# Sample block choice emitted before the last four projection tiles, key tiles first, and attention buffers placed in the normed input's tiles

## The chip, the cores and the metric

The kernel runs on one NeuronCore of a Trainium2 chip, as one program. Its engines are TensorE (PE: matmuls and transposes, fed by its own queue of weight loads, PEld), VectorE (DVE), ScalarE (ACT), GpSimd (POOL) and SyncE (SP, which here only issues transfers). ACT, SP and POOL each have a queue of DMA issues. The metric is the device time of one execution in microseconds (us); lower is better. The time before is the median of three executions.

## The reference, cut to what matters

One layer of a hybrid decoder is computed for 512 prompt tokens (one fresh sequence) and 8 samples of 4 new tokens each, whose past of 2048 tokens lies in page pools:

```python
x = x + 0.5 * swiglu1(rms_norm(x))             # FFN 1
z = rms_norm(x) @ w_in                         # one projection, columns split among the groups
o_nsa = nsa(z[..., :NSA_COLS])                 # 8 query heads in 2 groups, 2 K/V heads
o_rw  = rwkv7(z[..., NSA_COLS:])
x = x + concat([o_nsa, o_rw]) @ w_out
x = x + 0.5 * swiglu2(rms_norm(x))             # FFN 2
y = rms_norm_final(x)
```

The attention group has three branches, merged by sigmoid gates, each with a relative-position bias. The branch over compressed blocks attends to one K/V row for every 64 tokens, made by a small MLP. Its probabilities, summed over a group's heads, are the *importance* by which 16 blocks of 64 tokens are chosen for the second branch. The third is a window of 512 tokens:

```python
_, idx = lax.top_k(score, min(TOP_K_BLOCKS, n_blocks))   # score: importance; first and newest blocks forced
k_sel = gather_sample_blocks(cache_slc_k, ks, idx, page_table)
o_slc = slc_attend(q, pos, k_sel, v_sel, idx, valid, table)
```

For the prompt there are only 8 blocks, so all are chosen and no choice is computed.

## The kernel before

Numbers are fp32. Large products are made of three products of a high and a low part: `hh*wh + hl*wh + hh*wl` (`dense`, L152 to L155). The weights of a tile come in raw on SP's queue (`wload`, L137: tile `wraw`, three buffers of pool `wp`), ACT casts the high part `wh`, DVE subtracts to get the low part `wl`, three buffers each. The normed input lies in `hh` and `hl` (pool `hp`), 8 blocks of rows each.

The stages follow one another: FFN 1, `mix` (L338: input projection, RWKV group, attention group, output projection), FFN 2. In `mix` the attention group's projection goes tile by tile (`nsa_in`, L411) in the order of `ZORD`: 0 to 3 are queries, 4 and 5 the keys and values to be compressed, 10 the gates, then 6 and 8 the keys (selected branch, window) and 7 and 9 the values. A key tile is split into high and low parts `kk` for prompt scores (ACT L445, DVE L446). A value tile is transposed on PE (L434) into `vr`. Each of the four leaves the samples' 32 columns in `new`, by a copy on POOL (L428).

After tile 10 `prompt_cmp` computes the prompt's compressed branch (`PcmT`, `vcd`), then the last four tiles 7, 9, 6, 8 run. `attention_setup` follows: last product of the compression MLP (`hid`, `kccT`), query matrix `qb`, transposes of `new` into `vn`. `attention` (L947) runs two generators by turns: `sample_attn` (lane p) and `prompt_attn` (lane q), whichever is due by the costs that they yield (`STEP`). Their matmuls and transposes go through `mm` and `tr` (L949, L952), which keep the order in which they are written; where nothing is kept, the framework's scheduler orders each engine.

`sample_attn` first computes the samples' compressed scores and softmax (`Pc`), the importance `imp` (L1042), and its ranks, by four blocks of comparisons of all pairs (`gg`, L1065 to L1070, sums `cnt`), which give the mask `mb`. Then for each half of the samples, `scores(s)` multiplies five pairs of loaded pages with `qb`, DVE adds the mask and finds the minimum (`S`, `mx`, L1116), ACT takes the exponential (L1137), PE transposes (`PT`), and `values` multiplies with the pages. The pages come by `kv_load` (L964): 20 loads of eight 128 x 256 pieces, three as indirect DMAs on POOL (`gather`, L903), five on SP (L997), or as whole rows for the window (L986). `KVS` says into which buffers in turn: two of the attention pool (`kv`), the tiles of `hh` and `hl` once the projection is through, and `ar`.

`prompt_attn` works on 32 units: four blocks of 128 queries (i = 3 to 0), four heads (r) and two branches (b). A unit is scores on PE (`pS`), bias and minimum on DVE (L1350), exponential on ACT, normalising on DVE (L1356), transposes on PE (`pq`, into `PTp` or `PTo`), products with `vr` (`po`). Up to `LAG` = 3 units are scored ahead. The queries `qs` lie in `wl`'s buffers, some scores in `wraw`'s, and some transposed probabilities in `wh`'s. `w_out` splits the mixed rows `on` and `orw`, and runs eight tiles.

Of the kernel before, what the change touches and what calls it, by code (L numbers as in the profile page):

```python
# [17 lines left out]
KT = 8  # L18
# [3 lines left out]
STEP = 3.1  # L22
KVB = 4
ZORD = (0, 1, 2, 3, 4, 5, 10, 7, 9, 6, 8)
KVS = ("kv", "hh", "kv", "hl", "ar")
# [22 lines left out]
class Step:  # L48
# [289 lines left out]
    def mix(self):  # L338
        nc = self.nc
        r = self.norm_end()  # L340
        with ExitStack() as st:
# [533 lines left out]
    def attention_setup(self):  # L875
        nc, I, O = self.nc, self.I, self.O
        c = self.at
        self.on = c.tile([128, 4, 2, HW], F32, name="on")
        hg = self.hid
        nc.scalar.activation(hg, hg, AF.Gelu_apprx_tanh, bias=self.pb)  # L880
        self.kccT = c.tile([128, 8, 32], F32, name="kccT")
        pk = self.ps()
        nc.tensor.matmul(pk, self.w2[0:64], hg[0:64], start=True, stop=True)
        for g in range(2):
            gs = slice(64 * g, 64 * g + 64)
            nc.vector.tensor_copy(self.kccT[gs].rearrange("p n b -> p (n b)"), pk[gs, g:512:2])
        self.qb = c.tile([128, 8, 2, 4, 4], F32, name="qb")
        nc.vector.memset(self.qb, 0.0)
        for g in range(2):
            gs = slice(g * 64, g * 64 + 64)  # L890
            nc.vector.tensor_copy(self.qb[gs, :, g], self.zs[gs].rearrange("p r n t -> p n t r"))
        self.vn = c.tile([32, 2, 128], F32, name="vn")
# [61 lines left out]
    def attention(self, bias, cmp):  # L954
        todo = {"p": self.sample_attn(), "q": self.prompt_attn(self.kk, bias, self.vr, *cmp)}
# [15 lines left out]
    def kv_load(self):  # L971
# [4 lines left out]
        if t == "kv":  # L976
            kv = [self.at.tile([128, 4, 256], F32, name="kv", bufs=KVB) for j in range(2)]
        elif t == "ar":
            kv = [self.un1.tile([128, 4, 256], F32, name="kv", tag="ar%d" % j, bufs=1) for j in range(2)]
        else:  # L980
            x = self.hp.tile([128, 2, 4, 256], F32, name="kv", tag=t)
            kv = [x[:, j] for j in range(2)]
# [16 lines left out]
    def sample_attn(self):  # L999
        nc, I, O = self.nc, self.I, self.O  # L1000
        c, new, vn = self.at, self.new, self.vn
        self.pg = c.tile([1, 80], I32, name="pg")
        nc.sync.dma_start(self.pg, I["pg"])
        self.loaded, self.pairs = 0, []
        for _ in KVS:
            self.kv_load()
# [31 lines left out]
        yield 1  # L1038
        p = self.ps()
        self.mm(p[:, 0:64], gsum, Pf, start=True, stop=True)  # L1040
# [3 lines left out]
        self.tr(p[0:64, 0:128], Pf, self.ident)  # L1044
        PcT = c.tile([64, 128], F32, name="PcT")
        nc.scalar.activation(PcT, p[0:64, 0:128], AF.Copy)
        yield 1
        wb = self.rot.tile([128, 512], F32, name="wb", tag="r", bufs=1)
        nc.gpsimd.tensor_copy(wb[:, 0:384], t31.to_broadcast([128, 384]))
        nc.gpsimd.tensor_copy(wb[:, 384:512], sb[:, 0:128])  # L1050
        nc.gpsimd.tensor_add(wb[:, 0:4], wb[:, 0:4], mwin)
# [24 lines left out]
        yield 1  # L1076
        gr = c.tile([16, 48], F32, name="gr")
        p = self.ps()
        for hf in range(2):
            self.tr(p[0:16, 24 * hf:24 * hf + 24], self.gT[0:24, hf, 0:SW], self.ident[0:24, 0:24])  # L1080
        nc.scalar.activation(gr, p[0:16, 0:48], AF.Copy)
        yield 1
        p = self.ps()
        self.mm(p[:, 0:48], sel, gr, start=True, stop=True)
# [5 lines left out]
        for n in range(8):  # L1090
            for g in range(2):
                self.mm(pv[n // 4 * 32:n // 4 * 32 + 32, n % 4 * 128 + g * 64:n % 4 * 128 + g * 64 + 64],
# [502 lines left out]
```

## Time and profile before

| | |
|---|---|
| time before, median of 3 runs (lowest, highest) | 1404.97 us (1395.78, 1405.24) |
| profiled execution, its own time | 1392.31 us |
| its span in the trace | 1390.5 us |
| PE, DVE, ACT, POOL busy, share of the span | 95%, 51%, 37%, 19% |
| FFN 2, from 932.00 us to the end | 458.50 us |
| last four tiles' end to the first matmul of `w_out` | 783.80 us to 928.05 us |

The span is cut into stretches below. A busy time is the time in which an engine has an instruction running. A wait is idle time of an engine ahead of an instruction, put down to what released it. PEclk is the mean clock that TensorE was granted, as a share of full speed. In a timeline a row is one or several like instructions: start, time from the first's start to the last's end, and in brackets the idle time ahead.

### The profile page before, as it was taken

What the parts mean: (1) busy time and instruction counts of PE and PEld (TensorE: products, weight loads), DVE (VectorE), ACT (ScalarE), POOL (GpSimd) and SP (SyncE); (2) the same over time, 40 slices, a digit from 0 to 9 for tenths busy, and PEclk for the clock granted to TensorE, in tenths of its full rate; (3) what the DMA queues carried; (4) which work ended last, traced back from release to release, by engine and by line L of the source; (5) the groups of instructions that cost most, each with busy time, mean ns of one, the idle gap of its engine ahead of it and who ended that gap; (6) DMA issues with size and microseconds to landing.
All of it is one profiled execution on the core that took longest, in us unless ns stands there. A gap on an engine that the chain in (4) does not pass through costs nothing.

```text
span 1390.5 us, 31672 instructions
## 1 busy us (share of the span) xinstructions
PE 1315.2 (95%) x13313; PEld 1240.6 (89%) x13313; DVE 706.4 (51%) x1357; ACT 512.7 (37%) x925; POOL 258.9 (19%) x317
## 2 busy tenths in 40 slices
PE   6999999999999998998999779989999999999996
PEld 6999999999999977787678667769999999999996
DVE  6443343333333558869685675765544444442224
ACT  5232232233222555451223455754433333332231
POOL 2073567530000111210003214301000000000000
PEclk9999999999999999699999889999999999999998
DMA  4464465544443311112225528625322222233332
GB/s 157 162 197 121 149 201 186 174 132 116 124 118 114 112 54 46 34 41 73 73 78 180 149 72 243 201 79 179 100 92 84 91 86 90 88 100 108 102 105 84
DMA packets 99328, 163.25 MB, mean 117 GB/s; under 512 B 16185, under 2 KB 42881, under 8 KB 98546
## 3 DMA queue, kind: packets, MB, share of 16 engines
q1 hardware_dynamic: 74258, 114.71, 26.8%
q0 software_dynamic: 9040, 25.24, 6.1%
q10 hardware_dynamic: 15888, 21.28, 5.0%
q8 instruction: 105, 1.72, 0.5%
q14 instruction: 37, 0.30, 0.1%
HBM read 150.19 MB, written 16.72 MB: 120 GB/s over the span
## 4 chain that ended last, share of the span: by engine, by line
PE 68%; DVE 6%; ACT 3%; DMA 3%; issue 2%; POOL 0%; SPq 0%; ACTq 0%; DVEq 0%; POOLq 0%
PE acc L155 53%; PE pp L949 1%; PE pq L952 1%; PE po L949 1%; PE pS L949 1%; DMA kv<-in_slc 1%; PE pq L697 1%; PE pp L480 1%; PE pp L581 1%; DMA kv<-in_slc,idx 1%; DVE ivt L636 1%; PE pq L155 1%; PE pq L722 1%; PE pp L859 0%; DMA kv<-in_wkv 0%
## 5 line engine op out<-in xcount | busy, mean ns | idle before, releaser
L155 PE MATMUL acc<-hl,wh 128*128 128x272 f32 x2064 | 427.4, 292 | 3.9 <-ACT wh L146 3.9
L146 ACT ACTIVATE wh<-wraw 128x512 fp32r<-128x512 f32 x338 | 209.7, 621 | 581.9 <-PE acc L155 537.2
L155 PE MATMUL acc<-hh,wh 128*128 128x272 f32 x1808 | 384.1, 293 | 9.1 <-ACT hh L104 9.1
L148 DVE TENSOR_TENSOR wl<-wraw,wh 128x512 fp32r<-128x512 f32 x338 | 232.0, 687 | 306.2 <-ACT wh L146 304.3
L155 PE MATMUL acc<-hh,wl 128*128 128x272 f32 x1808 | 381.3, 292 | 1.6 <-DVE wl L148 1.6
L155 PEld LDWEIGHTS acc<-hl,wh 128*128 128x128 f32 x2064 | 325.3, 191 | 9.4 <-ACT wh L146 4.2
L155 PEld LDWEIGHTS acc<-hh,wh 128*128 128x128 f32 x1808 | 288.1, 190 | 14.5 <-ACT hh L104 9.1
L155 PEld LDWEIGHTS acc<-hh,wl 128*128 128x128 f32 x1808 | 285.5, 190 | 4.4 <-DVE wl L148 1.9
L903 POOL DMA_INDIRECT cp<-in_cmp,idx x128 | 131.1, 1024 | 98.6 <-issue 37.2
L122 POOL TENSOR_TENSOR ss<-ss,sq 128x544 f32<-128x544 f32 x23 | 31.6, 1374 | 612.4 <-ACT sq L118 597.0
L155 PE MATMUL acc<-ah,wh 128*128 128x272 f32 x660 | 136.9, 289 | 0.0
L155 PE MATMUL acc<-al,wh 128*128 128x272 f32 x660 | 136.3, 288 | 0.0
L155 PE MATMUL acc<-ah,wl 128*128 128x272 f32 x660 | 135.6, 286 | 0.0
L155 PEld LDWEIGHTS acc<-al,wh 128*128 128x128 f32 x660 | 104.0, 188 | 0.0
L155 PEld LDWEIGHTS acc<-ah,wl 128*128 128x128 f32 x660 | 103.3, 188 | 0.0
L155 PEld LDWEIGHTS acc<-ah,wh 128*128 128x128 f32 x660 | 103.0, 188 | 0.0
L190 DVE TENSOR_TENSOR u<-acc,r 128x544 f32<-128x544 f32 x42 | 30.4, 724 | 74.8 <-PE acc L155 74.8
L188 DVE TENSOR_TENSOR t<-acc,r 128x544 f32<-128x544 f32 x42 | 30.4, 724 | 74.1 <-PE acc L155 74.1
L903 POOL DMA_INDIRECT kv<-in_slc,idx x48 | 47.1, 982 | 108.8 <-DVE Y L730 60.3
L193 ACT ACTIVATE ah<-u 128x544 fp32r<-128x544 f32 x44 | 29.0, 658 | 64.1 <-DVE u L191 64.1
L194 DVE TENSOR_TENSOR al<-u,ah 128x544 fp32r<-128x544 f32 x44 | 31.9, 724 | 29.0 <-ACT ah L193 29.0
L1352 ACT ACTIVATE Sp<-Sp,st 128x512 f32<-128x512 f32 (+3 forms) x64 | 35.4, 554 | 9.1 <-DVE st L1350 7.4
(495 smaller groups left out, 1438.8 us busy)
## 6 DMA issues: line engine op xcount, KB each, us to landing
wraw<-in_wg SPq DMA_DIRECT2D x88, 256.0 KB
wraw<-in_wu SPq DMA_DIRECT2D x88, 256.0 KB
wraw<-in_wd SPq DMA_DIRECT2D x80, 256.0 KB
wraw<-in_win SPq DMA_DIRECT2D x50, 256.0 KB
kv<-in_slc SPq DMA_DIRECT2D x80, 128.0 KB
x<-xr ACTq DMA_DIRECT2D x16, 272.0 KB
xr<-x ACTq DMA_DIRECT2D x16, 272.0 KB
kv<-in_wkv SPq DMA_DIRECT2D x8, 512.0 KB
```

Source lines behind the costliest of these rows:

```text
L122: nc.gpsimd.tensor_add(self.ss, self.ss, sq)
L146: nc.scalar.activation(wh[:, :m], w[:, :m], AF.Copy)
L148: nc.vector.tensor_sub(wl[:, :m], w[:, :m], wh[:, :m].bitcast(F32))
L155: self.nc.tensor.matmul(p[h] if isinstance(p, list) else p[:, h, :HW], a, b[:, h], start=f, stop=l)
L188: nc.vector.tensor_mul(t, pt, r)
L190: nc.vector.tensor_mul(u, pu, r)
L193: nc.scalar.activation(ah[:, f], u, AF.Copy)
L194: nc.vector.tensor_sub(al[:, f], u, ah[:, f].bitcast(F32))
L480: self.nc.tensor.matmul(p[h][:, :b - a], lhsT, rhs[:, a:b], start=True, stop=True)
L903: self.nc.gpsimd.indirect_dma_start(out=tile[:, k], out_offset=None, in_=rows, in_offset=bass.IndirectOffsetOnAxis(ap=self.idx[:, k0 + k:k ...
L949: self.tc.keep_in_program_order(self.nc.tensor.matmul(*args, **kw))
L1352: nc.scalar.activation(S[g][:, :N], S[g][:, :N], AF.Exp, bias=st[:, g:g + 1], scale=-1.0, accum_out=st[:, 2 + g:3 + g])
```

## The change

`attention_setup` is cut in two. Its first half and the samples' choice of blocks, to the mask `mb`, the gates and `vcc`, become `sample_select`. It is called in `mix` after `prompt_cmp`, so ahead of the last four tiles, and its matmuls are left to the scheduler. `attention_rooms` is the second half, with room for the attention in `hh`'s and `hl`'s tiles (`ra`, `rb`) and in tag "Y" (`qy`). The last tiles come as 6, 8, 7, 9, a page load after each from the second on. With the queries, scores and transposed probabilities moved there, no attention buffer lies in `wp`. `STEP`, `KVS` and the places of `w_out`'s operands change too.

```diff
-STEP = 3.1
+STEP = 3.4
-ZORD = (0, 1, 2, 3, 4, 5, 10, 7, 9, 6, 8)
-KVS = ("kv", "hh", "kv", "hl", "ar")
+ZORD = (0, 1, 2, 3, 4, 5, 10, 6, 8, 7, 9)
+KVS = ("kv", "kv", "ar", "hh", "hl")
...
             cmp = self.prompt_cmp(*self.prompt_blocks())
-            for i in ZORD[7:]:
+            sel = self.sample_select()
+            bias = self.prompt_bias()
+            self.sample_pages()
+            for n, i in enumerate(ZORD[7:]):
                 self.nsa_in(i, r)
-            self.attention_setup()
-            bias = self.prompt_bias()
-            self.attention(bias, cmp)
+                if 0 < n:
+                    self.kv_load()
+            self.attention_rooms()
+            self.attention(bias, cmp, sel)
             self.w_out()
...
+    def attention_rooms(self):
+        nc, O = self.nc, self.O
+        self.on = self.at.tile([128, 4, 2, HW], F32, name="on")
+        self.qy = self.un.tile([128, 2, 512], F32R, name="qy", tag="Y")
+        self.ra = self.hp.tile([128, KT * 2 * HW], F32, name="ra", tag="hh")
+        self.rb = self.hp.tile([128, KT * 2 * HW], F32, name="rb", tag="hl")
+        self.vn = self.at.tile([32, 2, 128], F32, name="vn")
         pv = self.ps()
         for b in range(2):
             nc.tensor.transpose(pv[0:32, b * 128:b * 128 + 128], self.new[:, 1 + 2 * b], self.ident)
...
-                self.mm(p[32 * n:32 * n + 32, 32 * hf:32 * hf + 32], qbf[:, 4 * hf + n], self.kccT[:, 4 * hf + n], start=True, stop=True)
+                nc.tensor.matmul(p[32 * n:32 * n + 32, 32 * hf:32 * hf + 32], qbf[:, 4 * hf + n], self.kccT[:, 4 * hf + n], start=True, stop=True)
...
+        return mb, vb, nb, mwin, gate, PcT, vcc
...
+    def sample_attn(self, mb, vb, nb, mwin, gate, PcT, vcc):
...
+        while self.loaded < len(KVS):
+            self.kv_load()
...
-                PT = self.un.tile([128, 4, 128], F32, name="PT", tag="sg")
+                PT = self.rb[:, 2048 + 512 * (s % 2):2560 + 512 * (s % 2)].rearrange("p (j c) -> p j c", c=128)
...
-            yield 2 - hf
+            yield 1
...
-            if g and i % 2 == 0:
+            if i % 2:
+                q = self.qy[:, g]
+            elif g:
+                q = self.un.tile([128, 512], F32R, name="qs", tag="sg")
+            else:
                 q = self.rot.tile([128, 512], F32R, name="qs", tag="ss", bufs=1)
-            else:
-                q = self.wp.tile([128, 512], F32R, name="qs", tag="wl", bufs=WB[2])
...
-            S = [self.wp.tile([128, 512], F32, name="Sp", tag="wraw", bufs=WB[0]) for g in range(2)]
+            S = [self.rb[:, 3072 + 512 * g:3584 + 512 * g] for g in range(2)]
...
-        odd = self.at.tile([128, 2, 512], F32, name="PTo") if b else None
+        room = self.ra[:, 2048 + 1024 * b:3072 + 1024 * b]
...
-                t = odd[:, g] if b else self.wp.tile([128, 512], F32, name="PTp", tag="wh", bufs=WB[1])
+                t = room[:, 512 * g:512 * g + 512]
...
-        ops = [None] * 4 + [hl[:, 0], hl[:, 1], hl[:, 2]]
-        for k, t in ((7, "ar0"), (0, "ar1"), (1, "BK"), (2, "UV"), (3, "Y")):
...
+        ops = [hl[:, 2], None, None, None, None, None, hl[:, 0], hl[:, 1]]
+        for k, t in ((4, "ar0"), (5, "ar1"), (1, "BK"), (2, "UV"), (3, "Y")):
```

On PE, the end of the last projection tile (L155 are its matmuls) and the start of the attention read as follows before. L895 transposes `new`, L883 to L952 ahead of and behind it are the selection's first steps and prompt scores.

```order
L155 MATMUL acc<-hl,wh 128x272 x2
L155 MATMUL acc<-hh,wl 128x272 x2
L883 MATMUL pp<-hid,w_8816 128x512
L895 MATMUL pp<-ident,new 32x128 x2
L949 MATMUL pp<-kccT,qb 32x32 x8
L949 MATMUL pS<-kk,qs 128x512 x12
L949 MATMUL pp<-Pc,gsum 128x64
L952 MATMUL pp<-ident,Pc 64x128
L952 MATMUL pq<-ident,Sp 128x128 x8
```

After the change the same place reads:

```order
L1040 MATMUL pp<-Pc,gsum 128x64
L1044 MATMUL pp<-ident,Pc 64x128
L155 MATMUL acc<-hh,wl 128x272 x2
L155 MATMUL acc<-hh,wh 128x272 x2
L1074 MATMUL pp<-ident,gT 16x24 x2
L155 MATMUL acc<-hl,wh 128x272 x2
L155 MATMUL acc<-hh,wl 128x272 x2
L1077 MATMUL pp<-gr,sel 128x48
L1085 MATMUL pp<-w_8816,hid 32x64 x16
L438 MATMUL pp<-ident,z 128x128 x8
L888 MATMUL pp<-ident,new 32x128 x2
L942 MATMUL pp<-kv,qb 32x128 x16
```

The selection's matmuls have moved into the last tile; the transposes of both value tiles (`pp<-ident,z`) have moved behind it; and the transposes of `new`, which read tiles 7 and 9 (now the last two, before the first two of the four), stand ahead of the first sample scores (`pp<-kv,qb`) and of all prompt scores.

On POOL, the copies of the samples' columns (`new`, four tiles) and the indirect page loads at the same place read before:

```order
L428 COPY new<-z 128x32 x3
L903 DMA kv<-in_slc,idx 128x256 x3
L428 COPY new<-z 128x32
L903 DMA kv<-in_slc,idx 128x256 x3
L1049 COPY wb<-sb 128x384
```

and after:

```order
L432 COPY new<-z 128x32 x3
L896 DMA rb<-in_slc,idx 128x256
L896 DMA ra<-in_slc,idx 128x256 x3
L896 DMA rb<-in_slc,idx 128x256 x2
L432 COPY new<-z 128x32
L1102 COPY wb<-sb 128x384
```

The fourth copy, then of key tile 8 and now of value tile 9, stood between the two loads into `hh` and `hl`; now it stands behind both.

On DVE, what stands ahead of the first half's first masked scores. After the change, from the copy of the transposed `new` on (L1063 to L1065 are a rank block, L1340 the split of the next queries, L1361 biased prompt scores):

```order
L889 COPY vn<-pp 32x256
L1063 TENSOR_TENSOR gg<-gg,tri 128x225
L1340 SCALAR_TENSOR_TENSOR qs<-qd,qs 64x512
L1064 TENSOR_TENSOR gg<-gg 128x15x15
L1340 SCALAR_TENSOR_TENSOR qs<-qd,qs 64x512
L1065 TENSOR_REDUCE cnt<-gg 128x15
L1361 ISA Sp,st_9468<-pS,bias 128x512
L1361 ISA st_9468 128x1
L1066 TENSOR_SCALAR mb<-cnt 128x30
```

and before, from the same copy on:

```order
L896 COPY vn<-pp 32x256
L1029 TENSOR_TENSOR Pc<-pp,sb 128x64
L1030 TENSOR_REDUCE st<-Pc 128x2
L1350 ISA Sp,st_9362<-pS,bias 128x512
L1350 ISA st_9362 128x1
L1031 TENSOR_TENSOR Pc<-Pc,st 128x64
L1350 ISA Sp,st_9362<-pS,bias 128x512
L1350 ISA st_9362 128x1
```

The samples' softmax (`Pc`), all of the first rank block and most of the second have moved ahead of this copy; the end of the second and the last two rank blocks stand behind it still, among the biased scores.

## Rows read from the trace of the kernel before

**Rows 1.** The page of the profile, part 1: busy time of all engines, shares of the span and instructions.

```profile
PE 1315.2 (95%) x13313; PEld 1240.6 (89%) x13313; DVE 706.4 (51%) x1357; ACT 512.7 (37%) x925; POOL 258.9 (19%) x317
```

**Rows 2.** Busy time of each engine by stretch: the stretch in us, its length, PE, PEld, DVE, ACT and POOL busy (instructions), the granted clock, the share that DMA was busy, GB/s. The last two tiles end at 783.80, the first sample scores of the attention are transposed from 825.20, and its last matmuls end at 924.14.

```profile
740.00:783.80 43.80, 42.97 (x470) 40.41 (x469) 25.33 (x50) 17.99 (x29) 12.92 (x16) 1.00 0.56 171
783.80:825.20 41.40, 26.13 (x205) 18.73 (x204) 34.35 (x105) 20.40 (x48) 9.49 (x12) 0.76 0.41 110
825.20:924.14 98.94, 91.61 (x1214) 72.10 (x1214) 63.93 (x269) 64.06 (x191) 31.96 (x33) 0.96 0.58 177
924.14:932.00 7.86, 3.95 (x17) 3.74 (x18) 5.28 (x9) 4.34 (x8) 0.00 (x0) 0.57 0.43 131
932.00:1390.50 458.50, 446.13 (x3549) 444.75 (x3548) 190.88 (x274) 147.73 (x232) 17.82 (x13) 0.99 0.33 101
```

**Rows 3.** The same view for three shorter stretches in which the granted clock was low.

```profile
825.20:832.00 6.80, 6.11 (x82) 4.90 (x82) 1.45 (x4) 2.73 (x7) 1.93 (x2) 0.70 0.20 58
844.00:852.00 8.00, 6.83 (x77) 5.39 (x78) 2.63 (x11) 3.10 (x8) 2.84 (x3) 0.79 0.95 301
928.00:932.00 4.00, 3.95 (x17) 3.74 (x18) 1.77 (x3) 0.52 (x1) 0.00 (x0) 0.53 0.43 145
```

**Rows 4.** Waits of PE from 740 to 930 us: who waited, for what, us in total, times, the longest.

```profile
PE pp L952 <- ACT S L1137: 8.4, 3, 7.2
PE pS L949 <- DVE kk L446: 4.4, 3, 3.7
PE acc L155 <- ACT wh L146: 3.9, 1, 3.9
PE pp L949 <- DMA kv<-in_slc,idx: 3.3, 4, 1.1
```

**Rows 5.** Timeline of PE at the end of the tiles, and the selection's matmuls after it (start, us, instruction).

```profile
773.91 0.60 PE L434 MATMUL pp<-ident,z 128*128 128x128 f32 x4
...
775.20 0.66 PE L434 MATMUL pp<-ident,z 128*128 128x128 f32 x4
...
783.80 1.12 PE L883 MATMUL pp<-hid,w 64*128 64x512 f32 x2
...
784.85 0.39 PE L895 MATMUL pp<-ident,new 128*32 128x128 f32 x2
...
785.96 0.33 PE L949 MATMUL pp<-kccT,qb 128*32 128x32 f32 x16 [0.72 <-DVE kccT L886]
...
798.43 0.52 PE L949 MATMUL pp<-Pc,gsum 128*128 128x64 f32 x2
...
798.75 0.42 PE L952 MATMUL pp<-ident,Pc 128*64 128x128 f32 x1
```

**Rows 6.** Timeline of POOL behind the last tile: the first and the last two rows of the stretch of six page issues that holds one copy of `new`.

```profile
783.90 1.04 POOL L903 DMA_INDIRECT kv<-in_slc,idx  x1 [4.43 <-PE acc L155]
...
787.47 0.21 POOL L428 COPY new<-z 128x32 f32<-128x32 f32 x1
...
790.37 0.95 POOL L903 DMA_INDIRECT kv<-in_slc,idx  x1 [0.30 <-issue]
...
791.32 0.51 POOL L1049 COPY wb<-sb 128x384 f32<-128x384 f32 x1
```

**Rows 7.** The page loads by issuing engine: instructions, shortest, median and longest issue in ns, first and last start.

```profile
L903 POOL DMA_INDIRECT kv<-in_slc,idx x48: 944/948/1674, 739.4 to 892.5; - x48
```

**Rows 8.** Timeline of DVE: a biased prompt score, the last rank block from the sum ahead of it to the masked sample scores behind it (its first row, two of its comparisons, the scores), and a split of queries.

```profile
813.10 0.69 DVE L1350 CUSTOM_DVE_ANT_0 Sp<-pS,bias 128x512 f32<-128x512 f32 x1
...
818.44 0.62 DVE L1070 TENSOR_REDUCE cnt<-gg 128x15 f32<-128x450 f32 x1
...
819.09 0.40 DVE L1065 TENSOR_TENSOR gg<-imp 128x225 f32<-128x225 f32 x1
...
819.40 0.39 DVE L1066 TENSOR_TENSOR gg<-imp 128x225 f32<-128x225 f32 x1
...
823.61 0.68 DVE L1116 CUSTOM_DVE_ANT_1 S<-pp,mb 128x512 f32<-128x512 f32 x1
...
832.94 0.69 DVE L1329 SCALAR_TENSOR_TENSOR qs<-qd,qs 64x512 fp32r<-64x512 f32 x1
```

**Rows 9.** Timeline of PE ahead of the first transposes of sample scores: the last prompt units (scores `pS`, transposes `pq`, products `po`).

```profile
813.46 1.09 PE L949 MATMUL po<-PTo,vr 128*64 128x128 f32 x16
...
814.49 1.09 PE L952 MATMUL pq<-ident,Sp 128*128 128x128 f32 x8
...
815.33 1.18 PE L949 MATMUL pS<-kk,qs 128*128 128x512 f32 x4
...
816.44 0.49 PE L949 MATMUL po<-PcmT,vcd 64*128 64x128 f32 x2
...
816.86 1.09 PE L949 MATMUL po<-PTp,vr 128*64 128x128 f32 x16
...
825.20 1.11 PE L952 MATMUL pp<-ident,S 128*128 128x128 f32 x4 [7.25 <-ACT S L1137]
```

**Rows 10.** Timeline of PE at the end of the attention and the start of the output projection.

```profile
923.70 0.44 PE L949 MATMUL po<-PTo,vr 128*64 128x128 f32 x4
...
928.05 1.28 PE L155 MATMUL acc<-hl,wh 128*128 128x272 f32 x4 [3.91 <-ACT wh L146]
```

**Rows 11.** Timeline of SP's queue: the eight stores of the samples' new window values.

```profile
786.82 5.62 SPq L898 DMA_DIRECT2D out_owv<-vn  x8
```

More of the change, by code (lines that the diff above doesn't have):

```diff
@@ L980, in kv_load @@
         else:
-            x = self.hp.tile([128, 2, 4, 256], F32, name="kv", tag=t)
-            kv = [x[:, j] for j in range(2)]
+            room = self.ra if t == "hh" else self.rb
+            kv = [room[:, j * 1024:j * 1024 + 1024].rearrange("p (n f) -> p n f", f=256) for j in range(2)]
         self.pairs.append(kv)
@@ L997, in kv_load, with sample_select @@
             nc.sync.dma_start(kv[j][:, n], I["slc"][bass.ds(v, 1)].rearrange("a p f -> (a p) f"))
-    def sample_attn(self):
+    def sample_select(self):
         nc, I, O = self.nc, self.I, self.O
[L1001 to L1006, printed above, removed]
+        c = self.at
+        hg = self.hid
+        nc.scalar.activation(hg, hg, AF.Gelu_apprx_tanh, bias=self.pb)
+        self.kccT = c.tile([128, 8, 32], F32, name="kccT")
+        pk = self.ps()
+        nc.tensor.matmul(pk, self.w2[0:64], hg[0:64], start=True, stop=True)
+        for g in range(2):
+            gs = slice(64 * g, 64 * g + 64)
+            nc.vector.tensor_copy(self.kccT[gs].rearrange("p n b -> p (n b)"), pk[gs, g:512:2])
+        self.qb = c.tile([128, 8, 2, 4, 4], F32, name="qb")
+        nc.vector.memset(self.qb, 0.0)
+        for g in range(2):
+            gs = slice(g * 64, g * 64 + 64)
+            nc.vector.tensor_copy(self.qb[gs, :, g], self.zs[gs].rearrange("p r n t -> p n t r"))
         qbf = self.qb.rearrange("p n g t r -> p n (g t r)")
@@ L1037, in sample_attn @@
         Pf = P.rearrange("p h b -> p (h b)")
-        yield 1
         p = self.ps()
-        self.mm(p[:, 0:64], gsum, Pf, start=True, stop=True)
+        nc.tensor.matmul(p[:, 0:64], gsum, Pf, start=True, stop=True)
         imp2 = c.tile([128, 2, 30], F32, name="imp")
@@ L1043, in sample_attn @@
         p = self.ps()
-        self.tr(p[0:64, 0:128], Pf, self.ident)
+        nc.tensor.transpose(p[0:64, 0:128], Pf, self.ident)
         PcT = c.tile([64, 128], F32, name="PcT")
         nc.scalar.activation(PcT, p[0:64, 0:128], AF.Copy)
[L1047 to L1051, printed above, removed]
         nb = c.tile([128, 2, 32], F32, name="nb")
@@ L1079, in sample_attn @@
         for hf in range(2):
-            self.tr(p[0:16, 24 * hf:24 * hf + 24], self.gT[0:24, hf, 0:SW], self.ident[0:24, 0:24])
+            nc.tensor.transpose(p[0:16, 24 * hf:24 * hf + 24], self.gT[0:24, hf, 0:SW], self.ident[0:24, 0:24])
         nc.scalar.activation(gr, p[0:16, 0:48], AF.Copy)
-        yield 1
         p = self.ps()
-        self.mm(p[:, 0:48], sel, gr, start=True, stop=True)
+        nc.tensor.matmul(p[:, 0:48], sel, gr, start=True, stop=True)
         gx = c.tile([128, 6, 8], F32, name="gx")
```

41 lines of the change are left out of this document (14 added, 27 removed).

## The prediction

> **What bounds the kernel now.** The page's busy times come first: PE is busy 95% of the span [rows 1], so time can only be won where PE is not. The windows say where that is. Until 783.80 us PE is busy 42.97 of 43.80 us; from there to the first transposes of sample scores at 825.20 it is busy 26.13 of 41.40, at a granted clock of 0.76, while DVE is busy 34.35. In the rest of the attention PE is busy 91.61 of 98.94 us at 0.96, and from 924.14 to 932.00 only 3.95 of 7.86 at 0.57. FFN 2 behind it, 458.50 us, is full and untouched [rows 2]. The waits of PE name the causes: 7.2 us in one piece for the exponential of the first sample scores, 4.4 for the low halves of keys, 3.3 for page loads, 3.9 for `wh`, the first weights of `w_out` [rows 4]. The clock falls to about its lower level (1.2 of 2.4 GHz) where PE has stood idle: 0.53 of full from 928.00 to 932.00 [rows 3], behind 3.91 us of waiting [rows 10].
>
> So the stretch behind the last tile is limited by DVE, which has the samples' softmax and four rank blocks among the prompt's biased scores. Its last block starts behind the sum at 818.44, the masked scores start at 823.61 [rows 8], and PE transposes them 1.59 us later, at 825.20 [rows 9]. All the selection's work that DVE does before 783.80, where it is busy 25.33 of 43.80 us [rows 2], takes a piece off this stretch.
>
> **Step 1, the tiles' end.** PE takes in the selection's first matmuls: 1.12 us for the compression's last product, 0.33 for compressed scores, 0.52 and 0.42 for importance and its transpose; with the two small gate transposes, which I put at the 0.1 us that such a piece adds, 2.5. It gives out the transposes of two value tiles, 0.60 and 0.66 [rows 5]: +1.2. Whether PE waits inside the last tile for the softmax (`gsum` stands two blocks of weights ahead of its end) no row shows: from nothing to the 4.4 us that it waits now for DVE's key halves [rows 4]. DVE has 18 us free before 783.80 [rows 2] and the tile's first six blocks lie between, so I take 0.6. The tile ends at 785.6.
>
> **Step 2, a new hold.** Value tile 9 is now last, so the transposes of `new` wait for POOL's copy of it. That copy stands behind six indirect page loads into `hh` and `hl`, whose room comes free when PE ends the tile. Behind the tile of before, the six loads with one copy among them last from 783.90 to 791.32, 7.4 us, and the copy takes 0.21 [rows 6]: 785.6 + 7.4 + 0.2 = 793.2. With the transposes, 0.39 [rows 5], DVE can copy `vn` at 793.6. Queued behind the waiting PE row are all sample and prompt scores; behind the waiting `vn` on DVE stands the rest of the ranks. Without the hold both engines would be there at about 788, so it costs 5 us or more.
>
> **Step 3, DVE from `vn` to the masked scores.** The last stretch of before, 818.44 to 823.61, is 5.17 us, with two sums, five comparisons and the normalising of two units; it recurs whole. Ahead of it now stand `vn` (0.4, as a comparison), seven comparisons at 0.31 from start to start, another sum 0.62, six biased scores at 0.69, two query splits at 0.69 and one low half of `w_out`'s weights, also a pass over 512 columns, 0.69 [rows 8], and two small operations, 0.4: 0.4 + 2.2 + 0.6 + 4.1 + 1.4 + 0.7 + 0.4 = 9.8. Together 15.0: the scores start at 808.6, and PE transposes them at 810.2, not at 825.20: 15.0 us earlier.
>
> **Step 4, what PE still has to do.** The 98.94 us from 825.20 to 924.14 [rows 2] follow again, and with them what PE did before 825.20 and now has not done. By the order, three units are scored ahead of the first sample transposes, before it was seven, with four turned and three multiplied. A unit costs 1.11 to score (815.33 to 816.44), 0.84 to transpose (814.49 to 815.33), 1.03 to multiply (813.46 to 814.49) and, every second one, 0.42 for the compressed part (816.44 to 816.86) [rows 9]: 4 x 1.11 + 4 x 0.84 + 3 x 1.03 + 2 x 0.42 = 11.7. The attention ends at 810.2 + 98.9 + 11.7 = 920.8, **3.3 earlier**. This takes over all of that stretch's losses: 98.94 - 91.61 = 7.3 idle, and the low clock of two windows, 0.30 x 6.11 and 0.21 x 6.83 = 3.3 [rows 3]. They belong to the samples' chain, which is the same; that is why I keep them.
>
> **Step 5, the output projection.** Before, its raw weights wait for the buffers of `wp`, which hold prompt queries and probabilities to the end; PE's last `po` starts at 923.70, its next matmul at 928.05 after 3.91 idle [rows 10]. Now nothing of the attention lies there, and the first raw chunks stand on SP among the page loads, casts and low halves in the middle of the attention. What then comes last is the split of `on` behind the last unit, about 1.9 us of ACT and DVE passes (three at some 0.6 to 0.7, by [rows 8]), under the half of the first tile that uses `orw`: 4 matmuls take 1.28 us at the low clock [rows 10], so its 24 some 7, and half that at the full clock. So 3.9 us of waiting goes, and with it the low clock behind it, 0.47 x 4.00 = 1.9 [rows 3]: **5.8 earlier**. The price if this cover fails is the same 5.8.
>
> **Costed at nothing.** SP: behind five chunks of weights come the fifth load's first pieces, then the eight stores of `vn`, 5.62 us [rows 11], now from 794 to 800; the pages behind them land by about 809, needed from about 813, so 4 us of cover. ACT's store of new keys and the key halves move from behind the tiles to inside them, which takes the 4.4 us wait for them [rows 4] out of the stretch that step 3 recomputes.
>
> **The sum:** -3.3 - 5.8 = -9.1: the profiled span of 1390.5 would be 1381.4. That execution took 1392.31, 12.7 below the median of the three runs shown, so I set the difference on that median: 1404.97 - 9.1 = 1395.9, say 1396.
>
> **Rivals.**
>
> *The gain is larger, 1385.* The losses kept in step 4 come mostly from starved PE: the sample chain's latency with no prompt work beside it. With 11.7 us more prompt work in that stretch it could fill the 7.3 idle and keep the clock up, 3.3: -9.1 - 10.6 = -19.7. For it: 6.11 of 6.80 us busy at 0.70 just behind the long wait [rows 3]. Against it: the page loads' 3.3 us of waits [rows 4] don't go by more prompt work. A hold shorter by the 5 us of step 2 leads to the same side, and both together to -25.
>
> *Only the prefetch counts, 1399.* If DVE's rank blocks are delayed by more than step 3 has, S comes no earlier in relation to the work left: step 4 gives nothing, step 5 its 5.8. It needs 3.3 us more between tile and S, less than the upper bound of step 1's wait.
>
> *The stock of prompt work runs out, slower.* The samples' chain now starts with three scored units, before with seven scored. Its steps (minimum, exponential, transposes) leave gaps that PE filled from that stock; if each of the four units missing leaves a gap as long as the longest wait for key halves, 3.7 [rows 4], 14.8 us are lost: -9.1 + 14.8 = +5.7, 1411. It decides at 9.1 / 4 = 2.3 us a unit. Against it: DVE has 35 us and ACT 35 us free in the 98.94 [rows 2], and `LAG` keeps three units ahead.
>
> *POOL's issues take longer, about 1400.* The six loads of step 2 now run while DVE is in the middle of rank comparisons and key halves, and each us that they last longer is a us on S. The longest of 48 took 1674 ns against a median of 948 [rows 7]; six such give 6 x 0.73 = 4.4: -4.7. Break-even lies at 9.1 / 6 = 1.5 us more for each issue, which no row reaches.
>
> The Trainium skill, page "SBUF — State Buffer", in its warning on the "DVE blocks DMA" trap, says that a transfer issued from GpSimd has its descriptors written by GpSimd's own cores, and that these are locked out of a port shared with DVE while DVE runs certain fast modes, which an fp32 copy sets off. By that rule all six issues could wait out one DVE pass each, six passes of 0.69, and the sum would be -9.1 + 4.1 = -5.0. The trace agrees so far only that some issues are longer, 1674 ns at most; the median of 948 with DVE often busy speaks against a lock at every pass.
>
> **From these to the numbers.** Forecast (-14 to -5) 0.38, larger (-14 to -30) 0.36, only the prefetch (-5 to 0) 0.11, POOL's issues 0.06, stock runs out 0.09, of which 0.05 beyond +14. About 1%, 14 us, is what a measurement of this kernel can tell from no change. Faster by more: 0.36. Within: 0.38 + 0.11 + 0.06 + 0.04 = 0.59. Slower: 0.05. The likeliest is the forecast, 1396, by itself 1391 to 1400. The range is -30 to +4, 1375 to 1409: it leaves out a tail of the larger gain and most of the last rival, some 0.15.
>
> **What would show it.** Step 1: the last tile's matmuls end at 785 to 787. Step 2: PE idle ahead of the transposes of `new`, released by POOL's copy, at 793. Step 3: the first masked scores on DVE at 808 to 809. Step 4: the attention's last `po` at 920 to 921; at 905 to 912 the first rival holds, behind 924 one of the others. Step 5: no wait of PE for `wh` and a granted clock of 1.00 in `w_out`'s first microseconds. I am wrong if PE's waits inside the attention grow over 10 us, or if the page loads of POOL last beyond 796.

## The result, and the profile after

The changed kernel takes 1389.12 us (median of 20 runs, 1380.44 to 1400.55) beside 1399.95 for the kernel before in as many runs beside it: ratio 0.993, 95% interval 0.9906 to 0.9955, or 6 to 13 us, some 10 in the middle. That is a gain, and within 1%, as forecast; the sum of the prediction was 9.1 us. The profiled span fell from 1390.5 to 1380.2.

Two profiled executions differ by chance too, so the first thing to read is where they part. The change touches nothing ahead of the compression of the prompt's keys. Its first matmul, in the timeline of PE of the kernel before and then of the changed one:

```profile
744.96 1.11 PE L1218 MATMUL pp<-px,w1r 128*64 128x16 f32 x32 [0.83 <-issue]
```

```profile
740.87 1.11 PE L1227 MATMUL pp<-px,w1r 128*64 128x16 f32 x32 [0.97 <-issue]
```

So 4.09 us of the 10.3 are gone before the change can act. In two more executions on a chip of this speed (the last two experiments), this matmul came at 748.11 and 744.30, with nearly the same order of work ahead of it. The mean granted clock up to it was 0.98 in the two traces above and 0.97 in these two. From this matmul on the traces say 645.5 us before and 639.3 after: **-6.2**, at the edge of the timed interval. Everything below is counted from it: the first stretch reaches to the attention's last matmul (179.2 us before, 177.9 after: -1.3), the second from there to the end (466.4 and 461.4: -4.9).

The windows of the changed kernel, by the same events as in [rows 2]: to the tiles' end, to the first transposes of sample scores, to the attention's end, 8 us of the output projection, the rest (columns as there):

```profile
740.87:781.96 41.09, 40.70 (x452) 36.74 (x452) 27.53 (x58) 18.45 (x33) 10.72 (x12) 1.00 0.73 209
781.96:806.06 24.10, 12.29 (x88) 7.43 (x89) 19.18 (x59) 9.15 (x20) 9.20 (x12) 0.65 0.58 163
806.06:918.76 112.70, 103.10 (x1314) 82.14 (x1314) 74.45 (x303) 75.22 (x215) 31.77 (x33) 0.95 0.50 149
918.76:926.76 8.00, 7.31 (x58) 7.31 (x59) 4.36 (x8) 4.17 (x7) 0.00 (x0) 1.00 0.27 70
926.76:1380.20 453.44, 441.09 (x3508) 439.70 (x3507) 189.24 (x272) 146.44 (x230) 17.76 (x13) 0.99 0.33 101
```

The stretch that had PE busy for 26.13 of 41.40 us has become one of 12.29 of 24.10, and the one behind it has grown from 98.94 to 112.70. The output projection now starts at a granted clock of 1.00 where it had 0.57.

What DVE no longer does ahead of the masked scores is mostly prompt work. These are the windows from the tiles' end to the first masked scores, before and after, first with all engines (columns as in [rows 2]), then with the rank blocks alone (DVE busy, clock, DMA share, GB/s):

```profile
783.87:823.61 39.74, 26.06 (x203) 18.66 (x203) 33.66 (x103) 19.59 (x46) 8.83 (x12) 0.77 0.43 115
783.87:823.61 39.74, 9.70 (x24) 0.77 0.43 115
```

```profile
781.96:804.47 22.51, 12.29 (x88) 7.43 (x88) 17.66 (x53) 8.33 (x18) 8.53 (x12) 0.66 0.59 164
781.96:804.47 22.51, 9.16 (x23) 0.66 0.59 164
```

DVE's busy time falls by 16.0 us, but the rank blocks by only 0.5: they are emitted ahead of the last tiles and still run behind them. The biased scores and normalising of the prompt make 10.6 us of the 16.0 (14 of each before, 16.8 us; 6 and 4 after, 6.2 us); the rest is mostly the low halves of keys, the softmax and small passes. The prompt work has to be done later, and so the stretch behind grows.

PE's waits in the attention (columns as in [rows 4]):

```profile
PE pp L945 <- ACT S L1146: 7.0, 1, 7.0
PE pp L942 <- DMA kv<-in_slc,idx: 5.8, 4, 2.6
PE pp L888 <- POOL new L432: 4.2, 1, 4.2
...
PE acc L155 <- ACT on L1401: 0.7, 1, 0.7
```

The wait for the first sample scores is as long as before, 7.0 and 7.2 us. The wait for key halves, 4.4, is gone, and one of 4.2 for POOL's copy of `new` has come. Page waits grew from 3.3 to 5.8. The timeline of POOL shows the hold, six issues from 781.99 and the copy behind them:

```profile
781.99 1.18 POOL L896 DMA_INDIRECT rb<-in_slc,idx  x1 [3.70 <-PE acc L155]
...
789.59 0.22 POOL L432 COPY new<-z 128x32 f32<-128x32 f32 x1
```

and that of DVE shows that it stands 4.68 us ahead of `vn`, and then the start of the masked scores:

```profile
790.29 0.41 DVE L889 COPY vn<-pp 32x256 f32<-32x256 f32 x1 [4.68 <-PE pp L888]
...
804.47 0.68 DVE L1125 CUSTOM_DVE_ANT_1 S<-pp,mb 128x512 f32<-128x512 f32 x1
```

At the attention's end PE's timeline (as in [rows 10]) reads:

```profile
918.10 0.66 PE L942 MATMUL po<-ra,vr 128*64 128x128 f32 x8
919.45 0.77 PE L155 MATMUL acc<-hl,wh 128*128 128x272 f32 x4 [0.70 <-ACT on L1401]
```

The gap of 3.91 us is 0.70, and four matmuls take 0.77 us, not 1.28.

### The profile page after: what moved, and what is told of

The parts are those of the page before. It is cut to its first block, busy times and chain, and to the rows that moved or that the text cites. A ratio compares the mean times of both kernels' runs of the same rounds, so it can differ in the third digit from the quotient of the medians.

```text
span 1380.2 us, 31677 instructions
## 1 busy us (share of the span) xinstructions
PE 1312.3 (95%) x13313; PEld 1237.6 (90%) x13313; DVE 705.8 (51%) x1357; ACT 514.2 (37%) x925; POOL 259.5 (19%) x317
## 5 line engine op out<-in xcount | busy, mean ns | idle before, releaser
L155 PE MATMUL acc<-hl,wh 128*128 128x272 f32 x2064 | 426.6, 292 | 0.7 <-ACT on L1401 0.7
L155 PE MATMUL acc<-hh,wh 128*128 128x272 f32 x1808 | 384.3, 293 | 9.2 <-ACT hh L104 9.2
L155 PE MATMUL acc<-hh,wl 128*128 128x272 f32 x1808 | 380.9, 291 | 1.8 <-DVE wl L148 1.8
L155 PEld LDWEIGHTS acc<-hl,wh 128*128 128x128 f32 x2064 | 324.1, 190 | 6.3 <-issue 3.3
L155 PEld LDWEIGHTS acc<-hh,wh 128*128 128x128 f32 x1808 | 288.1, 190 | 14.6 <-ACT hh L104 9.2
L155 PEld LDWEIGHTS acc<-hh,wl 128*128 128x128 f32 x1808 | 285.2, 190 | 5.7 <-DVE wl L148 2.4
L155 PE MATMUL acc<-ah,wh 128*128 128x272 f32 x660 | 137.0, 289 | 0.0
L155 PE MATMUL acc<-al,wh 128*128 128x272 f32 x660 | 136.3, 287 | 0.0
L155 PE MATMUL acc<-ah,wl 128*128 128x272 f32 x660 | 135.5, 286 | 0.0
L155 PEld LDWEIGHTS acc<-al,wh 128*128 128x128 f32 x660 | 104.0, 188 | 0.0
L155 PEld LDWEIGHTS acc<-ah,wl 128*128 128x128 f32 x660 | 103.3, 188 | 0.0
L155 PEld LDWEIGHTS acc<-ah,wh 128*128 128x128 f32 x660 | 102.9, 188 | 0.0
L896 POOL DMA_INDIRECT kv<-in_slc,idx x36 | 35.4, 984 | 102.6 <-DVE Y L734 59.4
L1363 ACT ACTIVATE Sp<-Sp,st 128x512 f32<-128x512 f32 (+3 forms) x52 | 28.8, 555 | 15.5 <-DVE st L1361 14.1
```

The costliest lines, as they stand in the source:

```text
L155: self.nc.tensor.matmul(p[h] if isinstance(p, list) else p[:, h, :HW], a, b[:, h], start=f, stop=l)
L896: self.nc.gpsimd.indirect_dma_start(out=tile[:, k], out_offset=None, in_=rows, in_offset=bass.IndirectOffsetOnAxis(ap=self.idx[:, k0 + k:k ...
L1363: nc.scalar.activation(S[g][:, :N], S[g][:, :N], AF.Exp, bias=st[:, g:g + 1], scale=-1.0, accum_out=st[:, 2 + g:3 + g])
```

## The experiments

Ten of them ran on three other chips, on which every kernel is slower, the kernel before too (1527 to 1542 us); the last two on a chip where that takes 1399. Ratios are to the kernel before on the same chip with 95% intervals, traces are compared within one kind of chip. On the slower chips the changed kernel itself stands at 0.998 (0.9946 to 1.0015), a smaller gain than the 0.991 to 0.996 expected for it below. From the tiles' end to the attention's end it takes 159.4 us there, 136.8 on the first chip; 16 of the 22.6 us more are waits of PE for which the profile shows no releaser. Each trace is one execution, so differences of a few us between traces are weak evidence where the times do not bear them out.

**The choice behind the tiles again** (twice).

```diff
-            sel = self.sample_select()
-            bias = self.prompt_bias()
             self.sample_pages()
             for n, i in enumerate(ZORD[7:]):
...
+            sel = self.sample_select()
+            bias = self.prompt_bias()
             self.attention_rooms()
```

> The changed kernel with the samples' choice emitted behind the last tiles again (key tiles first, buffers in the normed input's tiles and all else as changed). Measured from the first matmul of the prompt's compression to the last matmul of the attention the kernel before takes 179.2 us and the changed one 177.9; from there to the end 466.4 and 461.4. My theory: the early choice is worth what DVE no longer does between the last tile and the first masked scores, less the prompt work postponed: compression product, softmax and two rank blocks, 6 to 9 us of chain, less about 5 us in which DVE now stands idle in the hold and 1 us of matmuls that leave the tiles: the first stretch is 180 to 182, the second stays 461.4, so 2 to 4 us slower than the changed kernel, ratio to before 0.995 to 0.997. Rival, only the prefetch counts: 177.9 and 461.4, ratio 0.993, no difference. Rival, the first masked scores' 15 us count in full: first stretch over 187.

> The samples' choice behind the last tiles again, a second time, beside the changed kernel. My theory, as before: the first masked scores 4 to 6 us later behind the tiles' end than in the changed kernel and the attention's end 2 to 5 us later, the output projection the same: ratio 0.3 points above that of the changed kernel. Rival, only the prefetch counts: the same as the changed kernel within 0.1 points.

Measured: 1.0015 (0.9981 to 1.005) and 1.0004 (0.9971 to 1.0036). The masked scores start 27.5 and 30.6 us behind the tiles' end, 23.5 in the changed kernel there, and the attention ends 162.8 and 164.6 us behind it (159.4). The second stretch is 461.3 and 462.9. So the early choice is worth 3.4 to 5.2 us by the traces, about what was expected (2 to 4), and some 0.3 points by the times (medians of 1529.2 and 1524.5 on the one chip that ran both), where the intervals overlap. The waits without a releaser in this stretch are 18.9 and 14.5 us, against 16.1 in the changed kernel, so the traces alone don't settle it. DVE's work between the tiles' end and the masked scores is 22.1 us in the first of them, against 17.6 in the changed kernel. That the hold takes back a part of the gain is argued, not shown: on these chips another wait stands in its place (see the run without it).

**Buffers put back into the weights' tiles, and the places of the operands** (three runs). Both parts of the change touch the start of the output projection.

```diff
-            if i % 2:
-                q = self.qy[:, g]
...
+                q = self.wp.tile([128, 512], F32R, name="qs", tag="wl", bufs=WB[2])
...
-                t = room[:, 512 * g:512 * g + 512]
+                t = room[:, 512 * g:512 * g + 512] if b else self.wp.tile([128, 512], F32, name="PTp", tag="wh", bufs=WB[1])
```

> The changed kernel with prompt queries, one in five of the score tiles and half of the transposed probabilities back in the weights' buffers. My theory: only the start of the output projection changes: PE waits for its first weights some 3.9 us and runs the first 4 us at a low clock; the second stretch (attention's end to the end) returns from 461.4 to about 466.4 and the first stays at 177.9: ratio to before 0.997 to 0.998. Rival, the early choice is all of the gain: second stretch stays near 461.4, ratio 0.993. Rival, the buffers in the weights' tiles also hold up units inside the attention: the first stretch is over 180 too, ratio 1.000.

Measured: 0.9979 (0.9939 to 1.0019), second stretch 462.1, PE's wait 1.2 us. My theory fell: with the buffers as before, nearly all of step 5's gain is still there. The attention, which I had not expected to change on this account, ends 154.1 us behind the tiles' end, 5.4 earlier than in the changed kernel; the tiles end later, so the first stretch is 198.0 where the changed kernel has 200.9. By this one trace the move of the buffers cost the attention some time; the ratios, 0.9979 and 0.998, show no difference. The order of ACT's work named the other part of the change: the places of the split operands, which let the second cast of weights go ahead of the four splits of `on`. Tried alone in the kernel before:

```diff
-        ops = [None] * 4 + [hl[:, 0], hl[:, 1], hl[:, 2]]
-        for k, t in ((7, "ar0"), (0, "ar1"), (1, "BK"), (2, "UV"), (3, "Y")):
...
+        ops = [hl[:, 2], None, None, None, None, None, hl[:, 0], hl[:, 1]]
+        for k, t in ((4, "ar0"), (5, "ar1"), (1, "BK"), (2, "UV"), (3, "Y")):
```

> The kernel before with one part of the change: only the places of the output projection's split operands are those of the changed kernel. With it ACT has two casts of the first weights ahead of the four splits of the attention's output, where the kernel before has one ahead and the other behind. My theory, from the run with the buffers put back, which lost only some 0.7 us at this place: the order on ACT and not the room in the weights' buffers made most of step 5; attention's end to the end falls from 466.4 to 461.5 to 462.5 us, PE's wait for the first weights from 3.9 to about 1.2, ratio to before 0.996 to 0.998. Rival, the room in the buffers was the cause: the wait stays 3.9, that stretch 466, ratio 1.000.

Measured: 0.9975 (0.9938 to 1.0012). The wait is 1.2 us, as expected, the second stretch 464.4, not 461.5 to 462.5: the granted clock is 0.60 in its first 8 us. With the buffers alone put back the same wait of 1.2 us is followed by a clock of 1.00, so the wait by itself does not explain the low clock. And both parts undone in the changed kernel:

> The changed kernel with two parts undone: prompt queries, scores and transposed probabilities back in the weights' buffers, and the operands of the output projection in their places of before. ACT's second cast stands behind the four splits again. My theory: PE's wait for the first weights is 3.5 to 4 us again and attention's end to the end 465.5 to 466.5, so 4 to 5 us more than the changed kernel's 461.4; the attention itself as in the changed kernel; ratio to before 0.998 to 1.002 on a chip where the changed kernel stands at 0.998. Rival, the order on ACT doesn't decide: 462, as with the buffers alone put back.

Measured: 0.9987 (0.9951 to 1.0022), second stretch 467.3, wait 3.9. The timelines of ACT show it, first with the places alone (in the kernel before), then with both undone:

```profile
1079.20 0.60 ACT L1390 ACTIVATE on<-po 128x512 f32<-128x512 f32 x1 [0.58 <-PE po L949]
1079.69 0.62 ACT L146 ACTIVATE wh<-wraw 128x512 fp32r<-128x512 f32 x1
...
1080.21 2.29 ACT L1400 ACTIVATE hl<-on 128x544 fp32r<-128x544 f32 x4
```

```profile
1077.42 0.60 ACT L1399 ACTIVATE on<-po 128x512 f32<-128x512 f32 x1
1077.91 0.62 ACT L146 ACTIVATE wh<-wraw 128x512 fp32r<-128x512 f32 x1
...
1078.43 2.29 ACT L1413 ACTIVATE hl<-on 128x544 fp32r<-128x544 f32 x4
1080.62 1.14 ACT L146 ACTIVATE wh<-wraw 128x512 fp32r<-128x512 f32 x2
```

PE's first matmul needs the second cast (`wload` casts blocks 0 to 3 first, and the projection starts with block 4). In the first timeline the second cast, at 1079.69, stands ahead of the four splits (the first had run at 1078.00); in the second only one cast does, and the other follows at 1080.62, behind 2.29 us of splits. So the places of the operands mend that, in the kernel before and in the changed one; with them as before, and the buffers as before, the wait is 3.9 us again. The room in the buffers adds 0.5 us to it (1.2 to 0.7). Whether the room alone, with the operands in their old places, would do as much was not run.

**The hold taken away.**

```diff
-        nc.gpsimd.tensor_copy(self.new[:, i - 6].rearrange("p (h t) -> p h t", h=2), z[:, :, 0:SW])
+        eng = nc.vector if i == 9 else nc.gpsimd
+        eng.tensor_copy(self.new[:, i - 6].rearrange("p (h t) -> p h t", h=2), z[:, :, 0:SW])
```

> The changed kernel with one copy moved: the samples' columns of value tile 9 are copied by DVE instead of POOL, so that they don't stand behind six page issues. My theory: PE's wait of 4.2 us ahead of the transposes of these columns goes, DVE's idle 4.7 us goes, the first masked scores start 4 to 5 us earlier behind the tile's end (22.5 us behind it now), and the attention ends 3 to 5 us earlier: first stretch 173 to 175, ratio 0.990. Rival, the hold is hidden by what comes later (PE's 7.0 us wait for the first masked scores grows, or page loads that now land later than they are wanted): first stretch 177 to 178, ratio 0.993.

Measured: 0.9961 (0.9924 to 0.9998); first masked scores 23.6 us behind the tiles' end, attention's end 159.5: as in the changed kernel on these chips (23.5 and 159.4), so by the number the rival holds. But there the changed kernel has another wait at this place, without a releaser in the profile: PE stands 4.66 us ahead of the transposes of the last value tile, and no longer for POOL. PE's timeline of the changed kernel on such a chip:

```profile
901.33 0.66 PE L438 MATMUL pp<-ident,z 128*128 128x128 f32 x4
906.64 1.11 PE L438 MATMUL pp<-ident,z 128*128 128x128 f32 x4 [4.66 <-issue]
908.17 0.58 PE L888 MATMUL pp<-ident,new 128*32 128x128 f32 x2 [0.41 <-issue]
```

With the copy on DVE, PE stood 4.0 us at the same place for the copy of the compressed values on ACT. In the changed kernel that copy ends at 906.59, 0.05 us ahead of PE's start at 906.64, so it is most likely the same wait under another name; what ACT waited for the profile does not say:

```profile
906.00 0.59 ACT L1088 ACTIVATE vcc<-pp 64x512 f32<-64x512 f32 x1 [7.13 <-remote]
```

So this run does not tell what the hold costs on a chip where that wait is absent.

**The second half's ranks later** (twice), **and both together.** The rank blocks become a function; the first half's are called where all were, the second half's behind the first half's second transposes, with a mask tile for each half.

```diff
+            for s in range(5):
                 PT, PN = turned(s, S, po)
+                if hf == 0 and s == 1:
+                    ranks(1)
                 yield 1
```

> The changed kernel itself, for a trace and a ratio on the same chip as the next three. On the chip of the first four experiments every kernel stood in long stretches without a cause that the profile shows, the kernel before too (1530 us), so their traces can't be set beside the first two. Expected, if the effect does not hang on the chip: ratio to before 0.991 to 0.996.

> The changed kernel with the rank blocks of the second half of the samples (two of four) moved behind the first transposes of the first half, and one mask tile for each half. My theory: two blocks of some 2.3 us leave DVE ahead of the first masked scores, which start 4 to 5 us earlier (18 us behind the tile's end, now 22.5); PE's 7.0 us wait for them shrinks to 2 to 3; the attention ends 3 to 5 us earlier, first stretch 173 to 175, ratio 0.990. Rival, PE's idle time only moves: page waits (5.8 us in all now) or the blocks' place among the later scores take it back, first stretch 177 to 178, ratio 0.993.

> The second half's rank blocks moved behind the first half's first transposes, a second time, beside the changed kernel. My theory: first masked scores some 15 us behind the tile's end (changed kernel 22.5), PE's wait of 7 us for them gone, the attention's end 3 to 6 us earlier, ratio 0.3 points below the changed kernel's. Rival, the idle time only moves: the attention ends within 1 us of the changed kernel's.

> The second half's rank blocks later, and value tile 9's sample columns copied by DVE in place of POOL. My theory: the hold of 4 us goes too, the first masked scores start 10 to 12 us behind the tile's end and the attention ends 6 to 9 us earlier than in the changed kernel: ratio 0.5 points below it. Rival, PE waits for the gate and compressed values' product (a wait for the samples' compressed values of some 4 us took the place of the hold when that copy alone was moved) or for pages: no gain over the rank blocks alone.

Measured: 0.9923 (0.9886 to 0.9959) and 0.9955 (0.9918 to 0.9993) for the ranks, 0.996 (0.9924 to 0.9995) for both. With the ranks alone the masked scores start 14.9 us behind the tiles' end in both traces and the attention ends 151.5 and 151.6 behind it, 7.8 us less than in the changed kernel, more than the 3 to 6 expected. With the copy moved too it is 150.9: hardly more, as the rival had it. PE waits for the masked scores no longer, here in the second of the two traces:

```profile
913.04 0.73 PE L942 MATMUL pS<-kk,qy 128*128 128x512 f32 x2 [0.56 <-DVE st L1368]
913.61 0.60 PE L945 MATMUL pp<-ident,S 128*128 128x128 f32 x4
```

The matmuls stand in the same order in these traces, and an earlier start of the masked scores by 8.6 us is an earlier end by 7.8. The times do not confirm it: beside the changed kernel on the same chip the medians are 1524.4 with the ranks later and 1524.5 without, and the intervals of the ratios overlap.

**More prompt work ahead of the first sample transposes.**

```diff
             probs(0, S)
-            yield 1
+            yield 1 if hf else 3
```

> The changed kernel with one number changed: the samples' generator yields 3 behind the first half's scores in place of 1, so that two prompt units are transposed, two more scored and one multiplied ahead of the first sample transposes. My theory: this work, 2 x 0.84 + 2 x 1.11 + 1.03 + 0.42 = 5.4 us of PE, then lies under the wait of 7.0 to 7.5 us for the first masked scores, which come at most 1 us later for one more biased score on DVE; the wait falls below 3 us and the attention ends 3 to 5 us earlier (tile's end to attention's end 155 to 157 where the changed kernel takes 159.4 on such a chip). Rival, it only moves: DVE's part of the two units (normalising, biased scores) delays the masked scores by as much as PE gains, and the attention ends within 1 us of the changed kernel's.

The change itself had lowered this number, from 2 in the first half to 1.

Measured: 0.9892 (0.9848 to 0.9936). The first stretch is 168.5 us (changed kernel on such a chip 177.9, before 179.2), the second 461.5. PE's waits and its windows between the tiles' end, the first sample transposes and the attention's end:

```profile
PE pp L888 <- POOL new L432: 4.2, 1, 4.2
PE pq L945 <- DVE Sp L1367: 2.4, 2, 1.8
...
PE pp L942 <- DMA kv<-in_slc,idx: 0.8, 1, 0.8
...
PE pp L942 <- DMA kv<-in_slc: 0.5, 1, 0.5
PE pp L942 <- DMA rb<-in_wkv: 0.5, 1, 0.5
```

```profile
789.57:815.92 26.35, 18.15 (x131) 11.62 (x131) 21.18 (x66) 13.45 (x30) 9.19 (x12) 0.81 0.47 137
815.92:916.63 100.71, 94.80 (x1274) 75.62 (x1272) 71.70 (x296) 70.70 (x206) 31.70 (x33) 0.98 0.57 169
```

The masked scores start 22.8 us behind the tiles' end, 0.3 later than in the changed kernel; the 7.0 us wait for them is gone, page waits fell from 5.8 to 1.8, and the clock is 0.81 and 0.98 where it was 0.65 and 0.95. The hold of 4.2 is still there. That is 9.4 us by this one trace, twice what I expected. Over the two windows PE is idle 7.3 us less (8.2 and 5.9, where it was 11.8 and 9.6) and busy 2.4 us less, at the higher clock. Why the page waits fall with it is not settled: the two long ones of the changed kernel lie at 872 and 882, among the scores of the samples' second half. By the times it is ahead of the kernel before by 0.6 to 1.5%, and ahead of the changed one only by medians of two sets of runs (0.9892 and 0.993, with overlapping intervals).

**The order of the tiles.**

```diff
-ZORD = (0, 1, 2, 3, 4, 5, 10, 6, 8, 7, 9)
+ZORD = (0, 1, 2, 3, 4, 5, 10, 7, 9, 6, 8)
```

> The changed kernel with the last tiles in the order of before, values first (7, 9, 6, 8). The transposes of the sample columns have both value tiles long before the end, so POOL's copy behind the page issues holds nothing; but the low halves of the last key tile come on DVE behind the end, and the prompt's scores wait for them as before (4.4 us). My theory: the one wait takes the other's place; the tile's end moves some 1 us later (value transposes are inside again), first masked scores within 2 us of the changed kernel's, the attention's end within 2 us. Rival, the key order is what the early choice needs: prompt scores 4 us later, and the attention ends over 3 us later. Rival, the hold was the greater loss: it ends over 3 us earlier.

Measured: 0.9923 (0.9881 to 0.9965), the changed kernel's own ratio. The first stretch is 174.5, 3.4 less than in the changed kernel, where I had expected it within 2 us: by the trace the last rival holds. Other waits stand in place of the hold:

```profile
PE pS L942 <- DVE mb L1066: 7.3, 1, 7.3
PE pS L942 <- DVE kk L450: 3.6, 2, 2.3
PE pp L1040 <- DVE Pc L1037: 2.9, 1, 2.9
...
PE pp L942 <- DMA kv<-in_slc,idx: 1.0, 2, 0.6
```

No gain of the key tiles first is to be seen, then; by this one trace they cost a little.

## Why the prediction was right, step by step

**Step 1, right.** The tiles end 41.1 us behind the first compression matmul, before 38.9: +2.2, predicted +1.8.

**Step 2, right.** The six issues take 7.6 us to the copy (7.4 predicted), the longest of them 1.18 us, so the rival of slow issues did not come true here, by either of the two reckonings given for it. PE stands 4.2 us for the copy, and DVE 4.7 us for `vn`. In the time of the trace before (4.09 us added) `vn` comes at 794.4, 0.8 later than predicted.

**Step 3, right.** From `vn` to the masked scores 14.2 us (15.0 predicted). Put into the time of the trace before, the scores start at 808.6 and are transposed at 810.2: both as predicted, though to the tenth only because this error of -0.8 and the +0.8 of step 2 cancel. Of the selection's work, which was to take a piece off this stretch, DVE did little more than the softmax ahead of the tiles' end; the rank blocks still ran behind it.

**Step 4, right in kind, and too large.** From the first transposes to the attention's end it is 112.7 us, predicted 98.9 + 11.7 = 110.6; counted from the common matmul the attention ends 1.3 us earlier, not 3.3. The 11.7 us of postponed work were right: PE is busy 11.5 us more. The term that was too small is the losses taken over: PE is idle 9.6 us in this stretch, not 7.3, and page waits are 5.8 us of that, not 3.3. That an earlier start of the masked scores pays only after the postponed prompt work is taken off was the point of the step, and the run with one other yield shows it from the other side: with two prompt units back ahead of the transposes the first stretch is 9.4 us shorter by one trace.

**Step 5, right in size, wrong in cause.** The second stretch fell by 4.9 us, predicted 5.8: PE's wait by 3.2 of the 3.9, and the rest is near the 1.9 that I put on the clock. I put it all on the room in `wp`. The runs show that the part I had not priced, the places of `w_out`'s operands, mends the order of ACT by itself, and that the room is worth some 0.5 us of the wait beside it. That the size came out is luck in so far as another part of the same change removed the wait.

**The rivals.** The larger gain needed the waits in the attention to go; in the changed kernel they stayed (7.0 for the masked scores, 5.8 for pages) and went only with the yield changed, which at 9.4 us comes near the 10.6 that this rival named. Only the prefetch: 4.9 of the 6.2 us of the traces are that, and 1.3 the attention, so on the trace it is nearer than I gave it credit for; the run with the choice behind the tiles again speaks against it with 3.4 to 5.2 us. The stock of prompt work did run out, as one rival had it, but once, at the wait for the masked scores, and that wait was there before with the same length. The sum of the prediction, 9.1, lies between the trace's 6.2 and the 9.8 of the times; no run tells which of the two is nearer to what the change is worth, so that it lies so near the times may be chance. `STEP` and `KVS` were not undone one by one, and the yield was not set back to its 2 of before, so what each of them adds to or takes from the 1.3 us of the attention stays open; by one trace each, the order of the tiles and the move of the buffers work against it.

## What to carry to other kernels

Work that is moved ahead of a stretch shortens it only by what then waits no longer: look at what the bound engine will do in the time set free, since here the same edit also took away the prompt work that had filled PE's wait, and one yield gave back 9.4 us of the first stretch in one trace. Work that is emitted earlier has not run earlier until the trace says so: here the rank blocks moved in the program and still ran behind the tiles. Before crediting a gain at a stage's start to free buffers, read the order of the casting engine there: an edit that seems to have nothing to do with it can move the one cast that PE waits for. When two traces are compared, find the last common event and count from it; 4 of 10 us were chance ahead of the change.

## What was not expected of the hardware

On three chips PE stood idle ahead of matmuls for which the profile shows no releaser ("issue"), in the first 400 us above all, which the first chip did not show. The dearest group of matmuls there, in the changed kernel, with the idle time ahead of it and what ended it:

```profile
L155 PE MATMUL acc<-hl,wh 128*128 128x272 f32 x2064 | 435.5, 295 | 29.0 <-issue 28.3 <-ACT on L1401 0.7
```

The same group on the first chip has 0.7 us of idle time in all. Over all products of weights these waits are 86.4 us in 80 pieces, every one in the first 400 us; ACT stands there too, 137.4 us ahead of ten casts of weights, for what the profile calls "remote". The kernel before takes 1527 us on such a chip, 1400 on the first, and the gain of the change is smaller there by the middle values, 0.998 and not 0.993, with intervals that overlap. What holds the engines there stays open.
